# Two-layer decoder trunk: high parts of a step ahead of its low parts, an earlier split, and 58 transfers on another queue

## Chip, cores and metric

One core of a Trainium2 chip runs the whole kernel in one launch. The metric is the device time of one execution in microseconds; lower is better. Everything is float32 in and out.

## What is computed

The input x has 1024 rows (the sequence) of 1024 features. Layer 0 is a gated linear recurrence; layer 1 is causal attention with a forgetting term, 16 heads of 64. The change touches layer 1 only, whose core is this:

```python
u = h @ w_in                                  # q, k, v, gate, f_logit
cum = cumsum(log_sigmoid(f_logit + b_f))      # one row per head
logits = q @ k.T / 8 + (cum[q] - cum[k])      # masked to k <= q
p = softmax(logits)
o = p @ v
y = (o * silu(gate)) @ w_out                  # x + y, then a last RMSNorm
```

## The kernel before

**Numbers in two parts.** A float32 operand is split for TensorE into a high part (rounded, `to_hi`, on ACT) and a low part (the rest, `to_lo`, on DVE or POOL). A product of two split operands takes three matmuls, hh x wh, hh x wl, hl x wh. Of the attention weights p, the parts are called ph and pl, and each piece of p takes two matmuls with v: ph and pl.

**One head.** `maxima(hd, c)` computes the scores of half c of the queries: four row tiles i (i = 7, 6, 5, 4 for c = 1; 3, 2, 1, 0 for c = 0) of 128 queries by (i + 1) x 128 keys. For each: matmuls into the PSUM tile S from T (k in high and low part, with rows of cum) and U (q); DVE masks S and takes the row maximum m in one instruction; ACT writes p = exp(S - m) and the row sums. `weigh(hd, c)` then turns p and multiplies by v into the PSUM tile O. Two of the four row tiles (the "mine" pieces) are turned by TensorE (the transposes pt); the other two (the "far" or returned pieces, in tile pp) are turned in 32 x 32 blocks by DVE (`turn_row`), stored to device memory (turnd) and fetched back transposed. Steps of `weigh` are taken two units of up to 512 columns at a time: split into ph and pl, then, one step later, `products` issues the matmuls into O. Results go from O to yo by an ACT copy and a DVE addition.

**Sums.** After the last row tile of a head, the row sums are inverted, turned to rows (rc), stored (recd) and fetched back broadcast over 64 partitions (recb, `fetch_sums`). POOL multiplies the gate sg by recb (`scale`), and later yo by sg (`gated`). `store_y` splits yo into high and low part and stores both in y1d until the output projection reads them.

**What sets the order.** While a head's attention runs, TensorE is kept busy by fill work: the projections of the next heads' q, k and gate (PSUM tile gps, groups of six matmuls per fill step), in heads 3, 7 and 11 the next four heads' values (vps), and in heads 12 to 15 the output projection. A string per run sets the interleaving: "0" is one step of `weigh`, "1" one row tile of `maxima`, "." one fill step. Each head has two runs: the first pairs `weigh(hd, 0)` with `maxima(hd, 1)`, the second `weigh(hd, 1)` with `maxima(hd + 1, 0)`. `ORDER` holds the two strings for heads 0 to 11, `LAST` those for heads 12 to 15. The strings and the calls set the sequence in which work is recorded; a scheduler then places each instruction on its engine, and every engine works through its own list in order. Transfers started by `nc.sync` stand in SP's list; nothing is started from POOL. A transfer that waits for its data holds those behind it on the same list.

Of the kernel before, what the change touches and what calls it, by code (L numbers as in the profile page):

```python
# [23 lines left out]
HD = 64  # L24
EPS = 1e-6
GROUP = 2
ORDER = "1.0..1.10.1.0", "10..1.0.10.10.0"
LAST = "1..0.1..10..1..0", "10..1.0..10..1.0..0"
NEG = -1e30
PSUM = bass.MemoryType.PSUM  # L30
# [3 lines left out]
def f32(ap):  # L34
    return ap.bitcast(F32)
# [3 lines left out]
def trunk(ctx: ExitStack, tc: tile.TileContext, xt, w0, wg, wo0, pc, gn, gf, w1, wv, wf, bf, wo1, out):  # L39
    nc = tc.nc  # L40
# [15 lines left out]
    def matmul(*args, **kw):  # L56
        pe[0] = nc.tensor.matmul(*args, **kw)  # L57
        return pe[0]
# [25 lines left out]
    def to_hi(hi, src, eng, scale=None):  # L84
        if eng is nc.scalar:
            if scale is None:
                nc.scalar.copy(hi, src)  # L87
            else:
                nc.scalar.activation(hi, src, AF.Copy, scale=scale)  # L89
        elif eng is nc.gpsimd:  # L90
            nc.gpsimd.tensor_scalar(hi, src, 1.0 if scale is None else scale, 0.0, ALU.mult, ALU.add)
        elif scale is None:
            eng.tensor_copy(hi, src)
        else:
            eng.tensor_scalar(hi, src, scale, None, ALU.mult)

    def to_lo(lo, src, hi, eng):
        return eng.tensor_tensor(lo, src, f32(hi), ALU.subtract)  # L98
# [80 lines left out]
    with ExitStack() as l0:  # L179
# [289 lines left out]
        for h, cs in enumerate(halves):  # L469
            y = [tuple(z[:, cs] for z in p) for p in ys[-2:]]  # L470
# [27 lines left out]
    y1d = dram.tile([2, KT, 2, P, HALF], F32, name="y1d")  # L498
    cumd = dram.tile([HEADS, 2, SEQ], F32, name="cumd")
    recd = dram.tile([HEADS, 8, P], F32, name="recd")  # L500

    with ExitStack() as l1:
# [5 lines left out]
        T = [tu.tile([P, 2, SEQ], F32R, tag=f"T{s}", name=f"T{s}") for s in range(2)]  # L508
# [109 lines left out]
        def load(hd, cs=slice(0, SEQ), us=(0, 1)):  # L618

            pair, s = hd // 2, hd % 2  # L620
            rows = slice(s * HD, (s + 1) * HD)
            hi, lo = (f32(z[rows, cs]) for z in kq[pair, 1])
            nc.sync.dma_start(f32(T[s][:64, 0, cs]), hi)
            nc.sync.dma_start(f32(T[s][:64, 1, cs]), hi)
            nc.sync.dma_start(f32(T[s][64:, 0, cs]), lo)
            nc.sync.dma_start(f32(T[s][66:68, 1, cs]), cumd[hd, :, cs])
            for c in us:
                load_q(hd, c)

        def load_q(hd, c):  # L630
            s = hd % 2
            u = U[s][c]
            hi, lo = (f32(z[s * HD : (s + 1) * HD, halves[c]]) for z in kq[hd // 2, 0])
            nc.sync.dma_start(f32(u[:64, 0]), hi)
            nc.sync.dma_start(f32(u[64:, 0]), hi)
            nc.sync.dma_start(f32(u[:64, 1]), lo)
            nc.sync.dma_start(f32(u[64:66, 1]), cumd[hd, :, halves[c]])
# [75 lines left out]
        def row_tile(i, n):  # L713

            c, r = i // 4, i % 4 - 2
            if r < 0:
                return at.tile([P, n], F32, tag=f"p{i}", name="p", bufs=1)
            size = (4 * c + 3) * P
            if r:
                two_rows[c] = at.tile([P, 2 * size + P], F32, tag=f"pp{c}", name="pp", bufs=1)  # L720
            return two_rows[c][:, r * size : r * size + n]

        def by_dma(hd, c):
            return 0 < 2 * hd + c < 27
# [27 lines left out]
        def maxima(hd, c):  # L752

            s = hd % 2
            pair = hd // 2
            if c == 0:
                stats[hd] = at.tile([P, 16], F32, tag="sums", name="sums")[:, :8]
            sums = stats[hd]
            for i in reversed(range(4 * c, 4 * c + 4)):
                n = (i + 1) * P  # L760

                o_ = 192 if i == 4 else 0
                S = ps.tile([P, SEQ], F32, tag="S", name="S")[:, o_:]
                u = U[s][c]
                qs = slice(i % 4 * P, i % 4 * P + P)
                for lo_, hi_ in ((0, min(n, HALF - o_)), (HALF - o_, n)):
                    if hi_ <= lo_:
                        continue
                    hi_ = max(hi_, lo_ + 256)
                    matmul(S[:, lo_:hi_], u[:, 0, qs], T[s][:, 0, lo_:hi_], start=True, stop=False)  # L770
                    matmul(
                        S[:, lo_:hi_], u[:96, 1, qs], T[s][:96, 1, lo_:hi_], start=False, stop=True
                    )
                m = at.tile([P, 1], F32, tag="m", name="m", bufs=4)
                masked[0] = nc.vector.tensor_tensor_reduce(  # L775
                    S[:, :n], S[:, :n], mask[:, SEQ - n :], -1.0, -NEG, ALU.add, ALU.min, accum_out=m
                )

                p = ps_[i] = row_tile(i, n)
                seen[0] = nc.scalar.activation(  # L780
                    p, S[:, :n], AF.Exp, bias=m, scale=-1.0, accum_out=sums[:, i : i + 1]
                )
                if i % 4 > 1 and by_dma(hd, c):
                    turn_row(i, p)
                yield
            if hd == HEADS - 1 or c == 1:
                b0, b1 = (4 * c if hd == HEADS - 1 else 0), 4 * c + 4
                nb = b1 - b0
                sums = sums[:, b0:b1]
                nc.vector.tensor_scalar(sums, sums, 2.0, None, ALU.mult)  # L790
                nc.vector.reciprocal(sums, sums)
                tr = ps.tile([P, P], F32, tag="O", name="tr")
                nc.tensor.transpose(tr[:nb], sums, ident)
                rc = at.tile([8, P], F32, tag="rc", name="rc", bufs=1)
                nc.vector.tensor_copy(rc[:nb], tr[:nb])
                nc.sync.dma_start(recd[hd, b0:b1], rc[:nb])
                if hd > 13:
                    fetch_sums(hd, b0, b1)
                yield

        def fetch_sums(hd, b0=0, b1=8):
            pair, s = hd // 2, hd % 2
            if s == 0:
                recs[pair] = at.tile([P, SEQ], F32, tag="recb", name="recb", bufs=1)
            nc.sync.dma_start(
                recs[pair][s * HD : (s + 1) * HD, b0 * P : b1 * P],
                recd[hd : hd + 1, b0:b1].rearrange("o b q -> o (b q)").to_broadcast([HD, (b1 - b0) * P]),
            )
# [8 lines left out]
        def weigh(hd, c, sub=slice(0, HALF)):  # L817

            pair, s = hd // 2, hd % 2
            V = Vs[pair]  # L820
# [3 lines left out]
            O = ps.tile([P, HALF], F32, tag="O", name="O")[:, : sub.stop - sub.start]  # L824
# [21 lines left out]
            count = [0, 2 * sum(map(len, mine + away))]  # L846
# [3 lines left out]
            def products(units, parts, far):  # L850
                todo = []
                for unit, (ph, pl) in zip(units, parts):
                    at_ = 0
                    for j, q, w in unit:
                        cs = slice(at_, at_ + w)
                        (later if away and not far and j == b + 3 else todo).append((j, q, w, ph[:, cs], pl[:, cs]))
                        at_ += w
                if far:
                    todo[1:1] = later
                    later.clear()  # L860
                for j, q, w, *z in todo:
                    v = V[j][:, 2 * s : 2 * s + 2].rearrange("p a d -> p (a d)")
                    o = O[:, q - sub.start : q - sub.start + w]
                    for part in z:
                        matmul(o, v, part, start=count[0] == 0, stop=count[0] == count[1] - 1)
                        count[0] += 1

            held = None
# [52 lines left out]
        def store_y(hd, c):  # L921
            if hd % 2 == 0:
                return
            pair = hd // 2
            yo = yos[pair, c]
            yh = at.tile([P, HALF], F32R, tag="xp", name="yh", bufs=2)
            with tc.issue_after(seen[0].ins):
                to_hi(yh, yo, nc.scalar)
            with tc.issue_after(masked[0].ins):
                to_lo(yo.bitcast(F32R), yo, yh, nc.vector)  # L930
            for part, y in enumerate((f32(yh), yo)):
                nc.sync.dma_start(y1d[c, pair, part], y)

        def settle(hd):
            yield
# [22 lines left out]
        def late_q(hd):  # L958
            load_q(hd, 1)
            yield from ()  # L960
# [166 lines left out]
        for hd in range(HEADS):  # L1127
            pair = hd // 2
            if hd % 2 == 0:
                if hd < 12:  # L1130
                    fill = kq_units(pair + 1, ((1, (0, 1)), (0, (0,))))
                elif hd == 12:
                    pairs = ((0, 1), (2, 3), (4, 5), (6, 7))
                    todo = [(db, c) for two in pairs for c in range(2) for db in two]
# [11 lines left out]
            elif pair < 6:  # L1146
                fill = chain(kq_units(pair + 1, ((0, (1,)),)), late_q(hd + 1), g_units(pair + 1))
            first, second = LAST if hd > 11 else ORDER
            side = put_away(hd - 1) if 0 < hd < 13 else iter(())
# [112 lines left out]
```

## Time and profile before

| | us |
|---|---|
| median of 3 timed runs | 1110.45 |
| lowest, highest | 1110.2, 1111.71 |
| profiled execution, its own time | 1113.33 |
| its span in the profile | 1111.6 |
| TensorE (PE) busy in the span | 1088.2 |
| DVE, ACT, POOL busy | 785.4, 581.3, 175.2 |

All times below that carry a clock position are from the one profiled execution. A timeline row gives the start, the duration, the engine, the source line, the operation with the tiles it writes and reads, and in brackets how long the engine had been idle and what it waited for. "PEld" is TensorE's loading of weights, "SPq" the issue of a transfer on SP's list. Layer 1's heads run from about 500 us to 1080 us. Nearly every matmul has line L57, and every split L87, L89 or L98, because helpers issue them.

### The profile page before, as it was taken

What the parts mean: (1) busy time and instruction counts of PE and PEld (TensorE: products, weight loads), DVE (VectorE), ACT (ScalarE), POOL (GpSimd) and SP (SyncE); (2) the same over time, 40 slices, a digit from 0 to 9 for tenths busy, and PEclk for the clock granted to TensorE, in tenths of its full rate; (3) what the DMA queues carried; (4) which work ended last, traced back from release to release, by engine and by line L of the source; (5) the groups of instructions that cost most, each with busy time, mean ns of one, the idle gap of its engine ahead of it and who ended that gap; (6) DMA issues with size and microseconds to landing.
All of it is one profiled execution on the core that took longest, in us unless ns stands there. A gap on an engine that the chain in (4) does not pass through costs nothing.

```text
span 1111.6 us, 15903 instructions
## 1 busy us (share of the span) xinstructions
PE 1088.2 (98%) x5645; PEld 921.9 (83%) x5645; DVE 785.4 (71%) x1280; ACT 581.3 (52%) x1037; POOL 175.2 (16%) x120
## 2 busy tenths in 40 slices
PE   9999999999999999999999999999999999999997
PEld 7787888888888888988888888888888889888876
DVE  7888755876568687757788477875678765666645
ACT  8487345355453665545555355553555544444435
POOL 2322212111212201420010200202002020110110
PEclk9999999999999999999999999999999999999999
DMA  6111111111112113446767347675376763885445
GB/s 220 62 52 43 51 54 48 43 54 45 49 45 75 48 55 127 130 113 165 199 204 195 116 139 195 198 198 146 107 204 195 202 170 100 251 294 182 138 148 189
DMA packets 100919, 145.81 MB, mean 131 GB/s; under 512 B 25348, under 2 KB 53636, under 8 KB 100840
## 3 DMA queue, kind: packets, MB, share of 16 engines
q1 hardware_dynamic: 100840, 144.80, 44.2%
q8 instruction: 44, 0.72, 0.3%
q14 instruction: 35, 0.29, 0.1%
HBM read 83.48 MB, written 36.11 MB: 108 GB/s over the span
## 4 chain that ended last, share of the span: by engine, by line
PE 75%; DMA 8%; DVE 7%; issue 5%; ACT 3%; SPq 1%; POOL 1%; ACTq 0%; DVEq 0%; POOLq 0%
PE gps L57 24%; PE ops L57 16%; PE ups L57 10%; PE vps L57 8%; PE O L57 5%; PE S L57 4%; PE gate L57 3%; PE turn L57 2%; DMA pp<-turnd 2%; PE pt L61 2%; DMA wf<-in_w 2%; DVE pl L98 2%; DMA turnd<-turn 1%; DVE turn L735 1%; DVE S L775 1%
## 5 line engine op out<-in xcount | busy, mean ns | idle before, releaser
L57 PE MATMUL gps<-hh,wh 128*128 128x512 f32 x576 | 229.8, 399 | 0.3 <-ACT wh L87 0.3
L57 PE MATMUL gps<-hh,wl 128*128 128x512 f32 x576 | 226.2, 393 | 0.0
L57 PE MATMUL gps<-hl,wh 128*128 128x512 f32 x576 | 225.3, 391 | 0.0
L87 ACT CAST wh<-wf 128x512 fp32r<-128x512 f32 (+2 forms) x156 | 94.5, 610 | 152.6 <-PE gps L57 47.8
L98 POOL TENSOR_TENSOR wl<-wf,wh 128x512 fp32r<-128x512 f32 (+1 forms) x60 | 101.9, 1705 | 376.0 <-ACT wh L87 261.4
L57 PEld LDWEIGHTS gps<-hl,wh 128*128 128x128 f32 x576 | 108.5, 188 | 23.5
L57 PEld LDWEIGHTS gps<-hh,wl 128*128 128x128 f32 x576 | 108.8, 189 | 19.6 <-POOL wl L98 0.2
L57 PEld LDWEIGHTS gps<-hh,wh 128*128 128x128 f32 x576 | 108.7, 189 | 19.4 <-ACT wh L87 0.6
L815 POOL TENSOR_TENSOR sg<-sg,recb 64x512 f32<-64x512 f32 x32 | 44.1, 1397 | 494.9 <-DMA recb<-recd 494.9
L775 DVE CUSTOM_DVE_ANT_0 S<-S,mask 128x512 f32<-128x512 f32 (+7 forms) x128 | 97.1, 758 | 25.4 <-PE S L57 24.9
L780 ACT ACTIVATE pp<-S,m 128x512 f32<-128x512 f32 (+1 forms) x64 | 54.4, 850 | 76.8 <-DVE m L775 76.3
L57 PE MATMUL S<-T,U 128*128 128x512 f32 (+7 forms) x384 | 91.4, 346 | 0.0
L57 PE MATMUL O<-pl,v 128*128 128x256 f32 (+3 forms) x302 | 80.3, 301 | 10.8 <-DVE pl L98 10.5
L98 DVE TENSOR_TENSOR wl<-wf,wh 128x512 fp32r<-128x512 f32 x96 | 64.9, 677 | 30.7 <-ACT wh L87 30.5
L375 DVE TENSOR_TENSOR x<-x,ops 128x512 f32<-128x512 f32 x80 | 54.1, 680 | 40.7 <-PE ops L57 40.7
L57 PE MATMUL O<-ph,v 128*128 128x256 f32 (+3 forms) x302 | 80.1, 289 | 1.3 <-ACT ph L87 1.3
L57 PEld LDWEIGHTS S<-T,U 128*128 128x128 f32 (+1 forms) x384 | 68.2, 189 | 12.6 <-ACT pp L780 0.6
L57 PE MATMUL ups<-hh,wl 128*128 128x512 f32 x192 | 75.3, 392 | 0.8 <-POOL wl L98 0.8
L57 PE MATMUL ups<-hh,wh 128*128 128x512 f32 x192 | 75.5, 394 | 0.4 <-ACT hh L89 0.4
L57 PE MATMUL ops<-yh,wh 128*128 128x512 f32 x192 | 75.2, 392 | 0.0
L57 PE MATMUL ups<-hl,wh 128*128 128x512 f32 x192 | 75.1, 391 | 0.1
L57 PE MATMUL ops<-yh,wl 128*128 128x512 f32 x192 | 74.7, 389 | 0.0
(170 smaller groups left out, 2361.8 us busy)
## 6 DMA issues: line engine op xcount, KB each, us to landing
wf<-in_w SPq DMA_DIRECT2D x100, 256.0 KB
turnd<-turn SPq DMA_DIRECT2D x26, 448.0 KB
pp<-turnd SPq DMA_DIRECT2D x52, 224.0 KB
wf<-in_wo SPq DMA_DIRECT2D x64, 128.0 KB
U<-qkh SPq DMA_DIRECT2D x64, 128.0 KB
T<-qkh SPq DMA_DIRECT2D x28, 256.0 KB
turnd<-turn SPq DMA_DIRECT2D x13, 384.0 KB
pp<-turnd SPq DMA_DIRECT2D x52, 96.0 KB
```

Of the source, the lines that this page charges most:

```text
L57: pe[0] = nc.tensor.matmul(*args, **kw)
L61: pe[0] = nc.tensor.transpose(*args)
L87: nc.scalar.copy(hi, src)
L98: return eng.tensor_tensor(lo, src, f32(hi), ALU.subtract)
L375: nc.vector.tensor_tensor(x, x, pt, ALU.add)
L735: nc.vector.transpose(t[:, 0 if c else r].rearrange("p (m k q) -> p k m q", m=4, q=32), p[:, :n].rearrange("p (k m q) -> p k m q", m=4, q=32),
L775: masked[0] = nc.vector.tensor_tensor_reduce(S[:, :n], S[:, :n], mask[:, SEQ - n :], -1.0, -NEG, ALU.add, ALU.min, accum_out=m)
L780: seen[0] = nc.scalar.activation(p, S[:, :n], AF.Exp, bias=m, scale=-1.0, accum_out=sums[:, i : i + 1])
L815: nc.gpsimd.tensor_tensor(sg, sg, recs[hd // 2][rows, part], ALU.mult)
```

## The change

There are five edits. (1) `products` issues all high parts of a step, then all low parts; before, each piece's high and low part came as a pair. (2) The first string of `ORDER` changes, so that in the first run of heads 0 to 11 the split of the returned pieces is recorded one row tile and one fill step earlier. (3) The store of the inverted sums and the fetch of recb are started by POOL. (4) So are the stores of y. (5) k's high part goes to its two places in T by one transfer with a repeated source instead of two transfers.

```diff
-ORDER = "1.0..1.10.1.0", "10..1.0.10.10.0"
+ORDER = "1.0..10.1.1.0", "10..1.0.10.10.0"
...
-            nc.sync.dma_start(f32(T[s][:64, 0, cs]), hi)
-            nc.sync.dma_start(f32(T[s][:64, 1, cs]), hi)
+            nc.sync.dma_start(f32(T[s][:64, :, cs]), hi.unsqueeze(1).to_broadcast([HD, 2, hi.shape[1]]))
...
-                nc.sync.dma_start(recd[hd, b0:b1], rc[:nb])
+                nc.gpsimd.dma_start(recd[hd, b0:b1], rc[:nb])
...
-            nc.sync.dma_start(
+            nc.gpsimd.dma_start(
                 recs[pair][s * HD : (s + 1) * HD, b0 * P : b1 * P],
                 recd[hd : hd + 1, b0:b1].rearrange("o b q -> o (b q)").to_broadcast([HD, (b1 - b0) * P]),
             )
...
-                for j, q, w, *z in todo:
-                    v = V[j][:, 2 * s : 2 * s + 2].rearrange("p a d -> p (a d)")
-                    o = O[:, q - sub.start : q - sub.start + w]
-                    for part in z:
-                        matmul(o, v, part, start=count[0] == 0, stop=count[0] == count[1] - 1)
+                for part in range(2):
+                    for j, q, w, *z in todo:
+                        v = V[j][:, 2 * s : 2 * s + 2].rearrange("p a d -> p (a d)")
+                        o = O[:, q - sub.start : q - sub.start + w]
+                        matmul(o, v, z[part], start=count[0] == 0, stop=count[0] == count[1] - 1)
                         count[0] += 1
...
-                nc.sync.dma_start(y1d[c, pair, part], y)
+                nc.gpsimd.dma_start(y1d[c, pair, part], y)
```

Lines from L624 on have a number lower by one afterwards.

**DVE, head 5, first run.** The rows behind the mask of i = 6, from the first on a projection tile (gps); 128x768 and 128x640 are the masks of i = 5 and 4, 128x512 that of i = 3; ISA is the masking instruction and the read of its maximum m, pl the low parts of the returned pieces, wl and qkl those of a weight and of q. Before:

```order
L608 TENSOR_TENSOR gps_6116<-gps_6116,rs_3284 128x512
L775 ISA S,m<-S,mask 128x768
L775 ISA m 128x1
L735 STREAM_TRANSPOSE turn<-pp 128x7x4x32
L98 TENSOR_TENSOR wl<-wf,wh 128x512
L614 SCALAR_TENSOR_TENSOR qkl<-gps_6116,qkh 128x512
L775 ISA S,m<-S,mask 128x640
L775 ISA m 128x1
L98 TENSOR_TENSOR pl<-pp,ph 128x8x2x32
L98 TENSOR_TENSOR pl<-pp,ph 128x256
L790 TENSOR_SCALAR sums<-sums 128x8
L791 RECIPROCAL sums<-sums 128x8
```

After:

```order
L608 TENSOR_TENSOR gps_6107<-gps_6107,rs_3284 128x512
L734 STREAM_TRANSPOSE turn<-pp 128x7x4x32
L774 ISA S,m<-S,mask 128x768
L774 ISA m 128x1
L98 TENSOR_TENSOR pl<-pp,ph 128x8x2x32
L98 TENSOR_TENSOR pl<-pp,ph 128x256
L98 TENSOR_TENSOR wl<-wf,wh 128x512
L614 SCALAR_TENSOR_TENSOR qkl<-gps_6107,qkh 128x512
L774 ISA S,m<-S,mask 128x640
L774 ISA m 128x1
L774 ISA S,m<-S,mask 128x512
```

The two pl move from behind the mask of i = 4 (128x640) to ahead of it; turn moves ahead of the mask of i = 5, and the two small instructions on sums, which no longer follow here, stand behind the mask of i = 3.

**ACT, the same place.** From the exponential of i = 6 to that of i = 3; ph are the high parts of the returned pieces. Before:

```order
L780 ACTIVATE pp,sums<-S,m 128x896
L87 CAST wh<-wf 128x512
L89 ACTIVATE qkh<-gps_6116 128x512
L780 ACTIVATE p,sums<-S,m 128x768
L87 CAST ph<-pp 128x8x2x32
L87 CAST ph<-pp 128x256
L780 ACTIVATE p,sums<-S,m 128x640
L905 COPY yo<-O 64x512
L780 ACTIVATE pp,sums<-S,m 128x512
```

After:

```order
L779 ACTIVATE pp,sums<-S,m 128x896
L87 CAST ph<-pp 128x8x2x32
L87 CAST ph<-pp 128x256
L87 CAST wh<-wf 128x512
L89 ACTIVATE qkh<-gps_6107 128x512
L779 ACTIVATE p,sums<-S,m 128x768
L904 COPY yo<-O 64x512
L779 ACTIVATE p,sums<-S,m 128x640
L779 ACTIVATE pp,sums<-S,m 128x512
```

The two ph stand directly behind the exponential of i = 6, and the copy of O to yo stands ahead of the exponential of i = 4 (128x640) instead of behind it.

**PE, the same place.** From the last fill matmul ahead of the returned pieces to the transposes pt. Before:

```order
L57 MATMUL gps_6209<-hl,wh 128x512
L57 MATMUL O<-ph,v_5538 128x256
L57 MATMUL O<-pl,v_5538 128x256
L57 MATMUL O<-ph,v_5631 128x128
L57 MATMUL O<-pl,v_5631 128x128
L57 MATMUL O<-ph,v_5569 128x256
L57 MATMUL O<-pl,v_5569 128x256
L57 MATMUL O<-ph,v_5600 128x256
L57 MATMUL O<-pl,v_5600 128x256
L57 MATMUL S<-T_3592,U 128x512 x2
L61 MATMUL pt<-ident,p 128x128 x8
```

After:

```order
L57 MATMUL gps_6200<-hl,wh 128x512
L57 MATMUL O<-ph,v_5531 128x256
L57 MATMUL O<-ph,v_5624 128x128
L57 MATMUL O<-ph,v_5562 128x256
L57 MATMUL O<-ph,v_5593 128x256
L57 MATMUL O<-pl,v_5531 128x256
L57 MATMUL O<-pl,v_5624 128x128
L57 MATMUL O<-pl,v_5562 128x256
L57 MATMUL O<-pl,v_5593 128x256
L57 MATMUL S<-T_3592,U 128x512 x2
L61 MATMUL pt<-ident,p 128x128 x8
```

The four low products follow the four high ones. The block of ten in the second run changes in the same way. The head's own pieces (four products, between the matmuls of S for i = 5 and a fill group before) now stand right behind the S matmuls of i = 6.

**SP and POOL, one head.** SP's rows between the store of the inverted sums and the fetch of them, head 4, before:

```order
L796 DMA recd<-rc 8x128
L623 DMA T_3592<-qkh 64x1024
L624 DMA T_3592<-qkh 64x1024
L625 DMA T_3592<-qkl 64x1024
L742 DMA turnd_4011<-turn 128x768
L805 DMA recb<-recd 64x1024
```

POOL's rows for a pair of heads, after:

```order
L795 DMA recd<-rc 8x128
L804 DMA recb<-recd 64x1024
L814 TENSOR_TENSOR sg_4635<-sg_4635,recb 64x512 x2
L795 DMA recd<-rc 8x128
L804 DMA recb<-recd 64x1024
L814 TENSOR_TENSOR sg_4635<-sg_4635,recb 64x512 x2
L914 TENSOR_TENSOR yo<-yo,sg_4635 128x512 x2
L931 DMA y1d<-yh 128x512
L931 DMA y1d<-yo 128x512
L931 DMA y1d<-yh 128x512
L931 DMA y1d<-yo 128x512
```

On SP four transfers stood between the store and the fetch; on POOL the fetch follows the store, and the multiplies by the sums follow each fetch. The four stores of y stand ahead of the next pair's first store of sums.

**DVE at the end of the kernel.** The addition of the output projection to xp (L1016, after L1015) and the low part yhl of y. Before:

```order
L98 TENSOR_TENSOR pl<-pt,ph 128x384
L1016 TENSOR_TENSOR xp<-xp,ops_10317 128x512
L906 TENSOR_TENSOR yo<-yo,O 64x256
L98 TENSOR_TENSOR yhl<-yo,yhh 128x256
L1016 TENSOR_TENSOR xp<-xp,ops_10356 128x512
L1068 TENSOR_TENSOR res<-turn,grow 128x512
```

After:

```order
L98 TENSOR_TENSOR pl<-pt,ph 128x384
L1015 TENSOR_TENSOR xp<-xp,ops_10299 128x512
L905 TENSOR_TENSOR yo<-yo,O 64x256
L1015 TENSOR_TENSOR xp<-xp,ops_10338 128x512
L98 TENSOR_TENSOR yhl<-yo,yhh 128x256
L1067 TENSOR_TENSOR res<-turn,grow 128x512
```

The last xp moves from behind yhl to ahead of it.

## The prediction

> **What bounds the kernel now.** I read the page first, then the waits of TensorE over the attention layer, then the busy time by stretches, then the timeline of single heads. The page's head and its engine line:
>
> ```profile
> span 1111.6 us, 15903 instructions
> PE 1088.2 (98%) x5645; PEld 921.9 (83%) x5645; DVE 785.4 (71%) x1280; ACT 581.3 (52%) x1037; POOL 175.2 (16%) x120
> ```
>
> TensorE is 98% busy, so a change that adds or removes no product can gain only where PE stands still. The waits of PE and of its weight loads from 475 us on (total us, times, longest):
>
> ```profile
> PE O L57 <- DVE pl L98: 10.5, 24, 0.7
> PE turn L57 <- DVE xp L1016: 1.7, 1, 1.7
> PEld O L57 <- DVE pl L98: 18.2, 30, 1.0
> ```
>
> Nearly all of it is one wait: the products into O wait for DVE to finish a piece's low part pl. PEld's 18.2 us counts the weight load that is held ahead of the product; start against start the loss is larger than PE's 10.5. No DMA is in this list as a cause. Two stretches (us, then busy time of PE, PEld, DVE, ACT, POOL, the granted clock, DMA share, GB/s):
>
> ```profile
> 650.00:770.00 120.00, 115.34 (x640) 97.69 (x639) 94.24 (x181) 65.00 (x142) 16.36 (x12) 1.00 0.73 198
> 930.00:1060.00 130.00, 130.00 (x673) 110.41 (x672) 83.53 (x166) 60.23 (x128) 12.02 (x9) 1.00 0.65 209
> ```
>
> Heads 4 to 7 leave PE 4.7 us idle while DVE works 94.24 of 120; heads 12 to 14 leave none. The clock is 1.00 in both, so it is no term. What can be won is thus in heads 0 to 11, plus 1.7 us at the end.
>
> **The edits, one by one. (a) Earlier split of the returned pieces, c=0.** Head 5, before:
>
> ```profile
> 682.91 0.96 DVE L775 CUSTOM_DVE_ANT_0 S<-S,mask 128x768 f32<-128x768 f32 x1
> 683.79 1.11 DVE L735 STREAM_TRANSPOSE turn<-pp 128x896 f32<-128x896 f32 x1
> 684.83 0.65 DVE L98 TENSOR_TENSOR wl<-wf,wh 128x512 fp32r<-128x512 f32 x1
> 685.39 0.68 DVE L614 SCALAR_TENSOR_TENSOR qkl<-gps,qkh 128x512 fp32r<-128x512 f32 x1
> 686.00 0.82 DVE L775 CUSTOM_DVE_ANT_0 S<-S,mask 128x640 f32<-128x640 f32 x1
> 686.55 0.28 PE L57 MATMUL O<-ph,v 128*128 128x256 f32 x1
> 686.74 1.02 DVE L98 TENSOR_TENSOR pl<-pp,ph 128x512 fp32r<-128x512 f32 x2
> 686.90 0.79 ACT L780 ACTIVATE p<-S,m 128x640 f32<-128x640 f32 x1 [1.08 <-DVE m L775]
> 687.48 0.39 PE L57 MATMUL O<-pl,v 128*128 128x256 f32 x1 [0.65 <-DVE pl L98]
> 688.59 0.58 ACT L905 COPY yo<-O 64x512 f32<-64x512 f32 x1 [0.80 <-PE O L57]
> 688.86 0.60 PE L61 MATMUL pt<-ident,p 128*128 128x128 f32 x4
> ```
>
> DVE goes without a gap from the mask of i=5 (128x768) to the low parts; PE has issued its first high product at 686.55 and stands until 687.48. Against a pace of 0.12 us for a 256-column product (701.10 to 701.22 in the next fence) that is 0.81 us, and about 0.1 more at the next piece: 0.91 us. Eight of the c=0 runs lose this and heads 3, 7 and 11 about 0.3 each, by the same reading: 8 x 0.91 + 3 x 0.31 = 8.2 us. After, by the order, the two pl stand ahead of the 640-wide mask, and O's products find them done: that 8.2 is gone.
>
> But the DVE work is the same; what is late next is the mask of i=4. It now has the two pl in front (pitches 0.60 and 0.36 us: the pair's 1.02 less the overlap at its end), and the first link of the DVE chain starts 0.41 later, because four products of the head's own pieces now stand ahead of a group of projection products on PE. So the mask starts at about 686.00 + 0.41 + 0.96 = 687.37, its exponential 0.90 behind it (as 686.00 to 686.90) at 688.27, and the transposes pt, which need that row of p, 0.86 later (0.79 and the sending) at 689.13. Before, pt started at 688.86, with the wait in O already paid. The copy of O now stands ahead of that exponential on ACT; O would be done by 687.4, so it ends by about 688.2 and holds nothing. Net: +0.27 us in an odd head. An even head and heads 3, 7, 11 come to +0.25 by the same steps. Eleven heads: **+2.7 us**. Bounds: 0.91 better per head if pt is not held (-8.2), +0.5 per head if another DVE piece slips in front (+5.5).
>
> **(b) High parts first, c=1.** Head 5, second run, its block of ten products:
>
> ```profile
> 699.20 0.69 DVE L98 TENSOR_TENSOR pl<-pp,ph 128x512 fp32r<-128x512 f32 x1 [0.53 <-DMA wf<-in_wv]
> 699.45 0.29 PE L57 MATMUL O<-ph,v 128*128 128x256 f32 x1
> 699.95 0.38 PE L57 MATMUL O<-pl,v 128*128 128x256 f32 x1 [0.21 <-DVE pl L98]
> 700.02 0.69 DVE L98 TENSOR_TENSOR pl<-pp,ph 128x512 fp32r<-128x512 f32 x1
> 701.10 0.28 PE L57 MATMUL O<-pl,v 128*128 128x256 f32 x1
> 701.22 0.40 PE L57 MATMUL gps<-hh,wh 128*128 128x512 f32 x1
> ```
>
> Before, the second product waits for the first pl, and the block ends at 701.22. After, five high products fill 699.45 to 700.03, by when the first pl is done; two low pieces follow, and the last two need the second pl, done at 700.71. They go at 700.76 and 700.88, end 701.00: 0.22 us won, and the second pl is the wait that is left. Six such blocks give 1.3; in heads 2, 6, 10 a block of four gains some 0.16 beside it (1.1 for the three); in heads 3, 7 and 11 the waits of two blocks are longer and I put 0.45 a head (1.3). Sum **-3.7 us**, bounds -6 and -2.
>
> **(c) Heads 3, 7, 11.** There the products of the next values (vps) fill the gaps, and the new order puts two or three of them between a block's high and low parts. These heads lose most:
>
> ```profile
> 763.32 2.98 POOL L815 TENSOR_TENSOR sg<-sg,recb 64x512 f32<-64x512 f32 x2 [28.51 <-DMA recb<-recd]
> 763.51 3.08 DVE L98 TENSOR_TENSOR pl<-pp,ph 128x512 fp32r<-128x512 f32 x2 [0.16 <-ACT ph L87]
> 764.64 0.28 PE L57 MATMUL O<-ph,v 128*128 128x256 f32 x1
> 765.22 0.39 PE L57 MATMUL O<-pl,v 128*128 128x256 f32 x1 [0.30 <-DVE pl L98]
> 766.64 0.38 PE L57 MATMUL O<-pl,v 128*128 128x256 f32 x1 [0.69 <-DVE pl L98]
> 766.99 0.36 PE L57 MATMUL vps<-wh,hh 128*128 128x256 f32 x1
> ```
>
> The block of six from 764.64 takes 2.35 us to 766.99, where six paces of 0.12 are 0.71: 1.64 lost. I take **-2 us** for the three heads, from 0 to -4; the small blocks between are too irregular to work out closer.
>
> **(d) Transfers on POOL's queue.** The last rows show the danger: POOL's multiply by the sums ran beside the two pl, which took 3.08 us instead of the 1.02 that the same pair took at 686.74. The Trainium skill, page "SBUF — State Buffer", section "Who interferes with whom", says the same: a VectorE instruction with two SBUF inputs contends with a GpSimd instruction that reads SBUF; the trace agrees with 3.08 against 1.02. When POOL starts is set by the arrival of recb. Head 4, and the same two transfers in the chain at the end of the kernel:
>
> ```profile
> 664.67 0.28 SPq L796 DMA_DIRECT2D recd<-rc  x1
> 668.28 1.19 SPq L805 DMA_DIRECT2D recb<-recd  x1
> 672.19 1.03 DVE L98 TENSOR_TENSOR pl<-pp,ph 128x512 fp32r<-128x512 f32 x2 [0.49 <-ACT ph L87]
> 673.59 0.28 PE L57 MATMUL O<-ph,v 128*128 128x256 f32 x1
> 673.64 2.54 POOL L815 TENSOR_TENSOR sg<-sg,recb 64x512 f32<-64x512 f32 x2 [45.05 <-DMA recb<-recd]
> 1064.31 3.51 DMA recd<-rc
> 1067.84 2.73 DMA recb<-recd
> ```
>
> The multiply starts 0.4 us after the last pl is done (673.22). SP puts four other transfers between the two, so on POOL's queue the second goes as soon as the first has landed. Nothing in this trace shows a transfer issued by POOL. Bound from one side: the quiet chain's 3.51 + 2.73, which would start the multiply at 671.0; from the other: no earlier than now, or later if POOL is slow to issue. In the middle, 672.3, it falls on the last two pl, each slowed by about 1 us, and the six products at 673.59 wait 0.2 to 1.2 us: 0.7. In odd heads rc itself now comes about 2.5 us later on DVE, which moves the multiply behind the splits. Of six even heads I take half: 3 x 0.7 = **+2.1 us**, bounds 0 and +10. POOL's own work is no limit (16.36 us of 120). On POOL's queue the four stores of y stand ahead of the next head's recd; they wait for yh and yl, done before the sums. The even heads' copy into yo waits for such a store; it has some 1.5 us of room.
>
> By the skill's page "DMA: Bandwidth & Descriptors", section "Anatomy of one DMA — SWDGE (gpsimd) path", a transfer issued by GpSimd takes about 2.0 us plus bytes by 436 GB/s, 2.6 us for recb; an estimate from that alone starts the multiply about 669.3, and no run here shows it yet. That would be the first rival's case.
>
> **(e) SP's relief and k's one transfer.** 17 + 17 + 24 + 18 = 76 transfers fewer on SP. PE waits for none of SP's loads in these heads: 0. If that cover is gone and a load of T or U lands late, PE stands at S for as long.
>
> **(f) The end.** Rows of the turn stage:
>
> ```profile
> 1073.27 0.42 DVE L98 TENSOR_TENSOR yhl<-yo,yhh 128x256 fp32r<-128x256 f32 x1 [4.29 <-ACT yhh L87]
> 1073.72 0.69 DVE L1016 TENSOR_TENSOR xp<-xp,ops 128x512 f32<-128x512 f32 x1
> 1074.46 0.66 PE L57 MATMUL turn<-ident,x 128*128 128x128 f32 x4 [1.71 <-DVE xp L1016]
> ```
>
> PE waits for a PSUM buffer that xp frees, and xp stands behind yhl, which waited 4.29 us for the sums. After, xp is ahead of yhl on DVE: **-1.7 us**. If this wait comes back at the next buffer, nothing.
>
> **Sum:** +2.7 - 3.7 - 2 + 2.1 - 1.7 = -2.6 us. The profiled execution took 1113.33 us around its span of 1111.6, which gives 1110.7; the median of the timed runs, 1110.45, is 2.9 lower, and gives **1107.8 us**, -0.24%. About 0.2% (2.2 us) is what a measurement of this kernel can tell from no change.
>
> **Rivals.**
> - *The multiply falls on the splits in all even heads (slower).* With a transfer as quick as the quiet chain, POOL's multiply reaches back to the pl at 671.0, and the block of ten and the block of six both wait. At head 7's 1.64 us for six heads this is +9.8 in place of +2.1: +5.1, **1115.5 us**. It decides for slower once a head loses over 1.2 us. For it: every multiply starts the moment recb lands (45.05 us of waiting), and the margin now is 0.4 us. Against: POOL may take longer to issue than SP waited.
> - *No collision:* the sums land no earlier: -4.7, **1105.7 us**.
> - *The c=0 wait does not come back at pt.* Then (a) is -8.2 in place of +2.7: -13.5, **1097 us**. For it: DVE has 21% idle in these heads, in other places. Against: in the stretch shown it has none.
> - *The waits just move about:* every gain in (b), (c) is taken by the next link of a DVE that is the second bound: within 0.2%, about 1110.
>
> **Chances.** The sum as worked, with some collisions, 0.36 (its own range 1105 to 1111); collisions everywhere 0.22; none 0.17; c=0 kept 0.10; waits only moved 0.15. Faster by over 0.2%: 0.19 of the first, 0.16 of the third, 0.10, and 0.02 of the last: 0.47. Slower: 0.22 and 0.05 from the first, 0.02 of the last: 0.29. Same: 0.24. The range takes in the collisions above and part of the kept c=0 gain below: 1098 to 1117.
>
> **What would show it.** In the profile after: no wait of O for pl in the c=0 blocks, and instead a wait of pt for ACT's p (or its exponential) in heads 0 to 11, about 1.2 us each; blocks of ten in c=1 at 1.55 us from first product to the next group instead of 1.77; no wait of turn for xp; pl of over 1 us beside POOL's multiply in some even heads. Wrong I am if pt shows no wait (far faster), if the pl beside POOL are slow in most heads, or if recb lands so late on POOL's queue that the multiply falls into the next head's c=0 splits, or if PE comes to wait for T, U or weights.

## The result: slower by 0.34%

The changed kernel takes 1115.93 us (median of 10 runs, 1114.08 to 1118.02), the kernel before, timed beside it, 1112.36 us (10 runs). The ratio is 1.0034, 95% interval 1.0023 to 1.0045: 3.6 us slower, where 2.6 us faster was forecast. The time lies inside the range, the direction is wrong. The profiled execution has a span of 1115.1 us against 1111.6.

The page after, its head, its engine line and its queues:

```profile
span 1115.1 us, 15873 instructions
PE 1085.7 (97%) x5645; PEld 920.9 (83%) x5645; DVE 785.7 (70%) x1280; ACT 581.8 (52%) x1037; POOL 206.7 (19%) x178
q1 hardware_dynamic: 95480, 134.25, 40.7%
q0 software_dynamic: 3760, 10.56, 2.9%
```

The same 5645 matmuls, but PE now idles more. POOL's 58 transfers move 10.56 MB on a queue of their own and add 31.5 us to POOL's busy time, which is no limit. The waits of PE after, from 475 us on, answer the question where:

```profile
PE pt L61 <- ACT p L779: 13.0, 12, 1.4
PE O L57 <- DVE pl L98: 6.6, 14, 1.1
PE turn L57 <- DVE res L1067: 1.0, 1, 1.0
```

The wait of O for pl has shrunk, the wait of turn for xp is gone, and a wait that was not there before, pt for ACT's p, takes 13.0 us in twelve places, one for each of heads 0 to 11. Head 5's timeline after, the stretch that the prediction worked out:

```profile
686.79 1.02 DVE L98 TENSOR_TENSOR pl<-pp,ph 128x512 fp32r<-128x512 f32 x2
688.19 0.62 PE L57 MATMUL O<-ph,v 128*128 128x256 f32 x4
688.65 0.63 PE L57 MATMUL O<-pl,v 128*128 128x256 f32 x4
688.93 0.82 DVE L774 CUSTOM_DVE_ANT_0 S<-S,mask 128x640 f32<-128x640 f32 x1
689.12 0.63 PE L57 MATMUL S<-T,U 128*128 128x512 f32 x2
689.92 0.79 ACT L779 ACTIVATE p<-S,m 128x640 f32<-128x640 f32 x1
690.86 1.09 PE L61 MATMUL pt<-ident,p 128*128 128x128 f32 x8 [1.11 <-ACT p L779]
```

The two pl end at 687.8, before O asks for them, and O's eight products run through. But the mask of i = 4 stands behind them at 688.93, its exponential at 689.92, and pt, which PE could start at 689.6, starts at 690.86. From the first product into O to pt it is 2.67 us, where it was 2.31 (686.55 to 688.86).

Where the heads lose is seen from the distance between the starts of the first S product of i = 7 in one head and in the next, after less before:

| head | change, us |
|---|---|
| 0, 1, 4, 5, 8, 9 | -0.03, +0.27, +0.30, +0.31, +0.23, +0.28 |
| 2, 6, 10 | -0.09, -0.35, -0.35 |
| 3, 7, 11 | +1.17, +0.83, +1.94 |
| 12 to 15 | 0.0 each |

That is +4.5 up to head 12, and the end gives 0.9 back. Heads 3, 7 and 11 make 3.9 of it. The tables and waits here are comparable, since both profiles hold one stretch of lower clock in head 3 (granted clock 0.83 from 620 to 630 us). It falls on waiting products before and on working ones after, which is some 0.4 us of head 3's +1.17. Among the experiments' profiles some have that stretch there, some elsewhere, some not at all, so of those the times, not the spans, are compared.

### The profile page after: what moved, and what is told of

It reads as the page before. It is cut to its first block, busy times and chain, and to the rows that moved or that the text cites. A ratio compares the mean times of both kernels' runs of the same rounds, so it can differ in the third digit from the quotient of the medians.

```text
span 1115.1 us, 15873 instructions
## 1 busy us (share of the span) xinstructions
PE 1085.7 (97%) x5645; PEld 920.9 (83%) x5645; DVE 785.7 (70%) x1280; ACT 581.8 (52%) x1037; POOL 206.7 (19%) x178
## 3 DMA queue, kind: packets, MB, share of 16 engines
q0 software_dynamic: 3760, 10.56, 2.9%
## 4 chain that ended last, share of the span: by engine, by line
PE 80%; DVE 5%; DMA 5%; issue 5%; ACT 3%; SPq 1%; POOL 1%; DVEq 0%; ACTq 0%; POOLq 0%
PE gps L57 29%; PE ops L57 16%; PE ups L57 10%; PE vps L57 8%; PE S L57 4%; PE O L57 4%; PE pt L61 3%; PE gate L57 3%; PE turn L57 2%; DMA wf<-in_w 2%; DVE pl L98 2%; DVE S L774 1%; DMA turnd<-turn 1%; DMA pp<-turnd 1%; SPq L746 1%
## 5 line engine op out<-in xcount | busy, mean ns | idle before, releaser
L57 PE MATMUL vps<-wh,hh 128*128 128x256 f32 (+1 forms) x256 | 73.6, 288 | 0.2 <-DVE x L484 0.2
L57 PE MATMUL ops<-yl,wh 128*128 128x512 f32 x192 | 73.6, 389 | 0.0
L57 PE MATMUL vps<-wh,hl 128*128 128x256 f32 (+1 forms) x256 | 73.3, 287 | 0.0
```

## Experiments

All are timed beside the kernel before, in 6 or 12 runs each; the ratios are to it.

**High parts first, alone.**

```diff
-                    for part in z:
-                        matmul(o, v, part, ...)
+                for part in range(2):
+                    for j, q, w, *z in todo: ...
```

> The kernel before with one edit: high parts of a step first. Theory 1 (the new first string of ORDER makes the loss, by moving a wait from O to the transposes pt): this edit alone gains 4 to 6 us, 0.13 us in each of six blocks of ten (c=1), 0.43 in each of heads 2, 6, 10, and some 0.35 in each c=0 block, where three more high products fill the wait for the first pl; no wait of pt for p appears. Theory 2 (the loss comes from the transfers on POOL's queue): the same or more. Against both: if it gains under 2 us, the order inside a step only moves the waits.

1111.25 us, ratio 0.9992 (0.9980 to 1.0005): no change that can be told. The places named do gain: each of the eight c=0 blocks waits 0.56 us instead of 0.91, each block of ten 0.46 instead of 0.60. But most of the sum does not reach the time. In heads 3 and 7 the wait of O for ph ahead of a block grows from 1.3 to 2.5 us, and in head 10, which gives 0.6 us back, a pl falls beside POOL's multiply (1.5 us). Expected were 4 to 6 us, so the gain of an edit here is not the sum of its waits.

**The new string, alone.**

```diff
-ORDER = "1.0..1.10.1.0", "10..1.0.10.10.0"
+ORDER = "1.0..10.1.1.0", "10..1.0.10.10.0"
```

> The kernel before with one edit: the new first string of ORDER. Theory 1: slower by 5 to 8 us; the waits of O for pl in the c=0 runs are gone, 12 waits of pt for ACT's p (about 13 us) are there instead, and most of the net loss is in heads 3, 7, 11, at 1 us or more each. Theory 2: within 2 us of before, as the +0.25 us a head of the prediction says.

1122.14 us, ratio 1.0093 (1.0079 to 1.0107): 10 us slower, more than expected. Its waits:

```profile
PE pt L61 <- ACT p L780: 12.4, 12, 1.1
PE O L57 <- DVE pl L98: 7.1, 14, 1.3
PE turn L57 <- DVE xp L1016: 0.6, 1, 0.6
```

The wait of pt is this edit's, with every transfer still on SP. The loss is not mostly in heads 3, 7, 11, as expected, but in heads 1, 2, 4, 5, 6, 8, 9 and 10, 0.4 to 1.6 us each: without the high parts first, their second runs lose too.

**Sums and y on POOL's queue, alone.** (`nc.sync` to `nc.gpsimd` at the three places.)

> The kernel before with two edits: the store and fetch of the sums and the stores of y on POOL's queue. Theory 1: about 1 us faster, all of it at the end, where xp stands ahead of yhl; the multiplies by the sums start within 1 us of before. Theory 2: slower by 2 to 4 us, with pl of 1.5 us beside POOL's multiply in more heads than 3, 7, 11.

1113.2 us, ratio 1.0015 (1.0005 to 1.0024): about 1.6 us slower by the ratio, not 1 us faster, and less than theory 2's 2 to 4 us. On DVE the one difference in order is xp ahead of yhl at the end, so that swap comes from these transfers. What costs is head 6 (+1.3 us), on DVE and POOL:

```profile
731.30 2.98 POOL L815 TENSOR_TENSOR sg<-sg,recb 64x512 f32<-64x512 f32 x2 [3.69 <-DMA recb<-recd]
731.66 2.91 DVE L98 TENSOR_TENSOR pl<-pp,ph 128x512 fp32r<-128x512 f32 x2 [0.49 <-ACT ph L87]
```

The sums came about 1.5 us earlier against the splits than before and met the last pair of pl. That is term (d) of the prediction, found where only this edit is made; heads 2 and 10 lose 0.4 and 0.6 in the same way. The profiled execution took 1115.33 us, the longest of the twelve, so these losses are larger than those behind the median.

**k by one transfer, alone.** (The hunk of `load`.)

> The kernel before with one edit: k's high part to both places in T by one transfer. Both theories: no change that can be measured (within 1 us), since TensorE waits for none of T's transfers; a wait of S for T would show that the one transfer lands later than the two did.

1110.63 us, ratio 0.9983 (0.9971 to 0.9994): 1.9 us faster, a little more than expected. No wait of S for T shows in either profile. Its SP list has fewer rows ahead of the fetch of the sums, and the multiply meets fewer pl, two instead of three in head 3 and one instead of two in head 7; more than that was not isolated.

**A fill step ahead of pt.**

```diff
-ORDER = "1.0..10.1.1.0", "10..1.0.10.10.0"
+ORDER = "1.0..10.1.1.0", "1.0.1.0.10.10.0"
```

> The changed kernel, and in the second string of ORDER one fill step (six projection products, 1.4 us) ahead of the transposes pt instead of behind them. Theory 1 (pt waits only because DVE's order makes the exponential late; TensorE has other work to do meanwhile): the waits of pt for ACT's p, 13 us in 12, go to under 3 us, no new wait takes their place, and it runs 8 to 12 us faster than the changed kernel, 4 to 8 us faster than before. Rival (DVE is the bound of these heads, the wait only moves on): within 3 us of the changed kernel, with as much waiting for pl or for S.

1101.78 us, ratio 0.9899 (0.9882 to 0.9917): 11.3 us faster than before and some 14 us faster than the changed kernel, more than theory 1 expected. Head 5 in this kernel:

```profile
684.23 0.40 PE L57 MATMUL gps<-hh,wh 128*128 128x512 f32 x1
684.56 0.80 ACT L780 ACTIVATE p<-S,m 128x640 f32<-128x640 f32 x1
685.63 1.03 PE L61 MATMUL pt<-ident,p 128*128 128x128 f32 x8
```

The six projection products from 684.23 cover the exponential, and pt starts with no wait in brackets. The kernel's waits:

```profile
PE O L57 <- DVE pl L98: 4.5, 14, 0.9
PE pt L61 <- DVE pl L98: 2.5, 5, 0.7
```

The wait of pt for ACT's p, 13.0 us in the changed kernel, is gone; a wait of pt for pl, 2.5 us in five places, is new. So DVE was not yet the bound of these heads. PE stood because nothing else was queued ahead of pt.

**The old first string in the changed kernel, and with the fill ahead.** These complete a two by two.

```diff
 # changed kernel, but:
-ORDER = "1.0..10.1.1.0", "10..1.0.10.10.0"
+ORDER = "1.0..1.10.1.0", "10..1.0.10.10.0"     # old first string
+ORDER = "1.0..1.10.1.0", "1.0.1.0.10.10.0"     # and fill ahead of pt
```

> The changed kernel with the old first string of ORDER and all else as changed. Theory 1: 2 to 5 us faster than the changed kernel, about 1111 to 1114 us, with no wait of pt for p. Theory 2 (POOL's queue makes the loss): within 1 us of the changed kernel.

> The changed kernel with the old first string of ORDER, and the fill step ahead of pt in the second string. With the changed kernel, the one with the fill ahead (1101.8 us) and the one with the old first string alone, this is a two by two of first string and fill. Theory 1 (the new string trades a wait in O for one of pt, and only with a fill ahead of pt is the trade a gain): about as with the old first string alone, 1109 to 1113 us, with the c=0 blocks still waiting for pl (0.55 us in each of eight). Rival (the fill ahead is a gain of its own): 1104 us or less.

| | fill behind pt | fill ahead of pt |
|---|---|---|
| old first string | 1108.73 us, 0.9968 (0.9951 to 0.9984) | 1112.62 us, 0.9996 (0.9980 to 1.0012) |
| new first string | 1115.93 us, 1.0034 (1.0023 to 1.0045) | 1101.78 us, 0.9899 (0.9882 to 0.9917) |

Undoing the one string makes the changed kernel 7 us faster, more than expected, and a gain over before instead of a loss; theory 2 foresaw no change. With the old string the fill ahead gains nothing and is 4 us slower. These times also hold what POOL's multiply meets, which differs among the four kernels in heads 2, 3, 6, 7, 10 and 11. In the other six (0, 1, 4, 5, 8, 9) it meets no low part in any of the four. Their changes against before, measured as in the table by heads above and added up, are:

| heads 0, 1, 4, 5, 8, 9 together | fill behind pt | fill ahead of pt |
|---|---|---|
| old first string | -2.2 us | -2.3 us |
| new first string | +1.4 us | -4.5 us |

There the fill is worth nothing with the old string and 5.9 us with the new one. The two strings are one decision: the split moved early pays only with work for PE ahead of pt.

**The changed kernel with SP's queue.** (The three `nc.gpsimd` back to `nc.sync`.)

> The changed kernel with the sums and y stored and fetched by SP's queue as before. Theory 1: within 2 us of the changed kernel, the waits of pt for p (13 us) as there; the wait of turn for xp is back. Theory 2: at or below the kernel before, 1110 to 1112 us.

1117.02 us, ratio 1.0042 (1.0026 to 1.0058), no better than with POOL's queue. The wait of turn for xp is back (0.7 us), that of pt stays at 12.5 us. The queue of the transfers did not make the loss.

**No multiply by the sums in heads 0 to 12**, in the kernel before and in the changed one. The gate is then not scaled in these heads; transfers and all else stay.

```diff
-                nc.gpsimd.tensor_tensor(sg, sg, recs[hd // 2][rows, part], ALU.mult)
+                if hd > 12: nc.gpsimd.tensor_tensor(sg, sg, recs[hd // 2][rows, part], ALU.mult)
```

> The kernel before without POOL's multiply of the gate by the sums in heads 0 to 12; the transfers stay. Theory 3 (what heads 3, 7, 11 lose is set by POOL's multiply falling on the low parts): about 3 us faster than before, all of it in the second runs of heads 3, 7 and 11, and no pl over 0.75 us there. Rival (the order of the vps products makes the loss): less than 1 us.

> The changed kernel without POOL's multiply of the gate by the sums in heads 0 to 12. Theory 3: 6 us faster than the changed kernel, since both late low parts are hit in heads 3, 7 and 11 there (2.1 to 2.7 us each), and within 1.5 us of the kernel before without the multiply; so the difference between the two kernels is then nearly gone. Rival: it keeps its distance of 3 to 4 us.

Before without it: 1109.74 us, 0.9970 (0.9956 to 0.9983). After without it: 1110.28 us, 0.9978 (0.9965 to 0.9991). The kernel before gains 3.3 us and the changed one some 6 us, and their distance falls from 3.6 to about 0.5 us (0.9 by the ratios), less than the intervals can tell from nothing. So the meeting makes most of the distance, as far as these intervals tell. It does not make the forecast gain: without it the changed kernel is still no faster than the one before, and its waits of pt for p are still there (12.9 us). Here is head 7 of the changed kernel with the multiply:

```profile
764.50 2.53 POOL L814 TENSOR_TENSOR sg<-sg,recb 64x512 f32<-64x512 f32 x2 [3.96 <-DMA recb<-recd]
766.00 3.00 DVE L98 TENSOR_TENSOR pl<-pp,ph 128x512 fp32r<-128x512 f32 x2 [0.16 <-ACT ph L87]
766.22 0.52 PE L57 MATMUL O<-ph,v 128*128 128x256 f32 x3
767.11 1.60 POOL L914 TENSOR_TENSOR yo<-yo,sg 128x512 f32<-128x512 f32 x1
767.64 0.50 PE L57 MATMUL O<-pl,v 128*128 128x256 f32 x2 [0.90 <-DVE pl L98]
769.05 0.38 PE L57 MATMUL O<-pl,v 128*128 128x256 f32 x1 [0.91 <-DVE pl L98]
769.40 0.36 PE L57 MATMUL vps<-wh,hh 128*128 128x256 f32 x1
```

and the same place without it:

```profile
765.05 1.03 DVE L98 TENSOR_TENSOR pl<-pp,ph 128x512 fp32r<-128x512 f32 x2 [0.16 <-PE O L57]
```

The pair of pl takes 3.00 us beside POOL's two products, sg and then yo, and 1.03 alone; the block of six takes 3.18 us (766.22 to 769.40) where its pace is 0.71.

**A later fetch of the sums.** Two kernels with high parts first, k's one transfer, everything on SP, and in heads 2, 3, 6, 7, 10, 11:

```diff
-            with tc.issue_after(written[0].ins):
+            with tc.issue_after((fetched if hd % 4 > 1 and hd < 12 else written)[0].ins):
                 fetch_sums(hd)
```

With the old strings:

> The kernel before with the high parts first and k's one transfer, the old string of ORDER, all transfers on SP, and the fetch of the sums of heads 2, 3, 6, 7, 10, 11 queued behind the fetch of the returned pieces on SP, so that the multiply comes some 4 us later than the last low part. Theory 3: no pl over 0.75 us in these heads, 4 to 6 us faster than before, and faster than either edit alone. Rival: as the first edit alone, about 1 us faster than before.

1106.79 us, ratio 0.9943 (0.9925 to 0.9960): 6.3 us faster than before, a little beyond what was expected, where high parts first alone could not be told from no change and k's transfer alone gave 1.9. With the new string and the fill ahead:

> New first string, fill step ahead of pt, high parts first and k's one transfer as in the best kernel so far, but all transfers on SP, and the fetch of the sums of heads 2, 3, 6, 7, 10, 11 queued behind the returned pieces. Theory 3 (the multiply on POOL beside the low parts costs what is left in heads 3, 6, 7, 11): 1 to 4 us faster than with POOL's queue, 1098 to 1101 us, no pl over 0.75 us in those heads. Rival (later sums hold up POOL's products or the y of the next head, or the queue of SP): 1102 us or more.

1104.02 us, ratio 0.9925 (0.9910 to 0.9940): the longest pl in these heads is 694 ns, as expected, but it is not faster than the 1101.78 us with POOL's queue. Its waits:

```profile
PE O L57 <- DVE pl L98: 4.3, 15, 1.2
PE S L57 <- ACT pp L780: 3.9, 3, 1.5
```

S waits for an exponential, 3.9 us in three places (heads 2, 6 and 10), where the 1101.78 us kernel has 0.2 us. In heads 3, 7 and 11 DVE's turn waits for the store of the rows before it, in head 7:

```profile
738.78 1.11 DVE L735 STREAM_TRANSPOSE turn<-pp 128x896 f32<-128x896 f32 x1 [2.42 <-DMA turnd<-turn]
```

The rival's time holds: the collision is gone and other waits have come. That the later fetch makes them is not shown: this kernel differs from the 1101.78 us one in the queue too, and the kernel with the old string and the fill ahead, on POOL's queue and without the later fetch, also has 4.3 us of S waiting there.

## Why the prediction was wrong

Two steps failed, and heads 3, 7 and 11 are where both did. By the two profiles, with the first run of a head taken from the first S product of i = 7 to pt and the second from pt to the next head (us; what (d) and (e) did to the heads lies within the first three rows):

| term | said | measured |
|---|---|---|
| (a) first runs, heads 0 to 11 | +2.7 | +6.3 |
| (b) second runs of the other nine heads | -2.4 | -2.3 |
| (b) and (c) second runs of heads 3, 7, 11 | -3.3 | +0.5 |
| (d) POOL's queue in heads 0, 2, 4, 6, 8, 10 | +2.1 | none hit |
| (f) the end | -1.7 | -0.9 |
| sum | -2.6 | +3.6 |

**(a), the earlier split: right in mechanism, the size wrong by 3.6 us.** Head 5 went nearly as worked out: pt comes 0.36 us later than before, where 0.27 was said, with O's wait gone. From the first product into O to pt, heads 2, 4, 6, 8, 10 have +0.29 each and heads 1, 5, 9 +0.36: 2.5 us, where the working has 2.1. The first step that failed is "An even head and heads 3, 7, 11 come to +0.25 by the same steps", for heads 3, 7 and 11. Head 7, before and after:

```profile
745.39 0.28 PE L57 MATMUL O<-ph,v 128*128 128x256 f32 x1
747.11 1.04 PE L61 MATMUL pt<-ident,p 128*128 128x128 f32 x8
```

```profile
744.63 1.11 DVE L734 STREAM_TRANSPOSE turn<-pp 128x896 f32<-128x896 f32 x1 [0.83 <-DMA turnd<-turn]
746.99 0.62 PE L57 MATMUL O<-ph,v 128*128 128x256 f32 x4
749.91 1.09 PE L61 MATMUL pt<-ident,p 128*128 128x128 f32 x8 [1.37 <-ACT p L779]
```

Before, O to pt took 1.72 us there, with only 0.31 us of waiting in it; after, 2.92. These heads had 0.31 to win and paid the same wait at pt as the others, and in heads 7 and 11 turn, now ahead of the mask of i = 5, waits some 0.85 us for a store besides. They lose 0.96, 1.21 and 1.27, 3.4 us in place of 0.75. The working's own numbers would have said most of it: its new wait is 0.91 + 0.27 = 1.18 us a head, and against 0.31 to win that leaves +0.87, not +0.25. Head 0, not counted, loses 0.1. Over the whole first runs (a) comes to +6.3 in place of +2.7. That this string decides the sign is shown by the changed kernel with the old one, which is faster than before (0.9968).

**(b), high parts first: right for nine heads.** The blocks of ten gained 0.13 each, not 0.22, in heads 0, 1, 4, 5, 8, 9; heads 2, 6, 10 gained 1.5 together, not 1.1. Sum -2.3 against -2.4.

**(b) and (c) in heads 3, 7, 11: no gain.** -1.3 and -2 were said. The blocks of the second runs lost 6.0 us before and 7.6 after, and a wait of O for ph ahead of a block, 1.3 us, went away; with the lower clock in head 3 it comes to +0.5. This is the second step that failed: the working treated the spread of vps as cover; it did not ask whether POOL's multiply would still meet the last pl. It does, beside sg and then beside yo. In the profiles without the multiply these blocks lose some 3.5 us less in the kernel before and some 5.9 less in the changed one. The meeting takes the gain away; the loss itself is in the first runs, and stays without it.

**(d), POOL's queue: the right mechanism at the wrong place.** +2.1 was put on heads 0, 2, 4, 6, 8, 10. None of them is hit. Head 4 after, on POOL and DVE:

```profile
666.74 0.53 POOL L795 DMA_DIRECT2D recd<-rc  x1 [3.22 <-DVE rc L794]
669.16 0.55 POOL L804 DMA_DIRECT2D recb<-recd  x1 [1.89 <-DMA recd<-rc]
673.90 1.03 DVE L98 TENSOR_TENSOR pl<-pp,ph 128x512 fp32r<-128x512 f32 x2 [0.49 <-ACT ph L87]
674.85 2.54 POOL L814 TENSOR_TENSOR sg<-sg,recb 64x512 f32<-64x512 f32 x2 [5.14 <-DMA recb<-recd]
```

A transfer's issue takes POOL 0.53 us, and the fetch goes 2.4 us after the store instead of 3.6. But the fetch then took 5.7 us to the multiply, as long as SP's (668.28 to 673.64, 5.4), and the multiply still starts only as the last pl ends (674.9). The estimate worked out in the prediction from the Trainium skill's page "DMA: Bandwidth & Descriptors" ("Anatomy of one DMA — SWDGE (gpsimd) path") is 2.6 us for recb; this case's trace does not agree, with 5.7 us from the issue to the multiply, and the measurement decides. With POOL's queue alone, the collision does come, in heads 2, 6 and 10.

**(e)** 0 was said; k's transfer alone measured -1.9 us (-3.2 to -0.7), as large as several terms that were worked out.

**(f), the end.** -1.7 was said; -0.9 came between the two profiles, and turn now waits for res (1.0 us in the waits after), a possibility that the text named. That the swap gives even 0.9 is not shown. From head 15's first S product of i = 7 to the end it is 69.6 us before and 68.7 after, but also 68.5, 68.5 and 68.8 in the kernels with high parts first alone, the new string alone and k's transfer alone. These keep the old order there and wait 0.5 to 0.8 us for xp. The 1.7 us of the profile before was the longest such wait in any of these profiles.

Of the rivals, the one on the slower side had the time nearly right (1115.5 against 1115.93) and the engine pair right, but in other heads, and its sum had no more than 2.7 us for pt. That its time agrees is luck.

## What to carry to other kernels

When work on a busy second engine is moved ahead, write down what it is moved ahead of, and give the first engine something to do until that is ready; the changed kernel, with no fill ahead of the next consumer, lost 0.3%, and with one fill step there gained 1.0%. Work such a step out for every kind of iteration, above all for the ones that had no wait to remove: they pay the new wait in full. Where two engines slow each other, take the one away in an experiment on both kernels; the difference between them then shows how much of the loss is the meeting's and how much the edit's own.

## What the runs showed of the hardware

A low part pl of returned pieces (128x512, both inputs in SBUF) takes about 1.5 us on DVE beside POOL's multiply instead of 0.69. Whether they meet turns on differences of 0.1 to 2 us: the multiply moved from behind the splits onto them, or back, with nearly every edit, even those that do not touch it.

A stretch of 3.4 us at half clock, 0.83 over 10 us, appears in some of the profiles at 620 to 630 us, in some elsewhere, in some not at all. In the kernel before (PE's busy time stands first behind a stretch's length, the granted clock third from the end):

```profile
620.00:630.00 10.00, 9.27 (x61) 8.54 (x61) 8.02 (x11) 4.30 (x11) 5.77 (x4) 0.83 0.36 98
617.40:620.80 3.40, 2.00 (x13) 1.39 (x11) 2.26 (x6) 2.55 (x8) 1.85 (x2) 1.00 0.49 153
620.80:624.20 3.40, 2.92 (x8) 2.46 (x9) 3.40 (x4) 0.93 (x3) 3.17 (x2) 0.50 0.69 176
```

It is worth about 1.7 us (half of 3.4), as much as several of the edits, so spans of single profiles can differ by that much. It does not come at any place. Seven of the fourteen profiles hold eight such stretches in the heads, and each begins where PE has just stood: PE was busy for 1.4 to 2.0 of the 3.4 us ahead of it, five times beside the late low parts of head 3. Standing alone does not bring it: the profile of the new string alone has 1.00 from 620 to 630 us, with PE busy for 1.38 of the 3.4 us from 621.2.
